# The first sub-layer of a two-layer decoder trunk: where its adaLN shift and scale are computed, and in which order its weights are loaded

## The chip, the core and the metric

The kernel runs on one core of one Trainium2 chip. The time is the device time of one execution in microseconds (us): 1291.8 us, the median of 3 runs (1289.95 to 1295.27). The core has a matrix engine (PE in the profile; its weight loads are shown apart as PEld), VectorE (DVE), ScalarE (ACT), GpSimd (POOL) and SyncE (SP), which here only issues loads. Each engine takes its own list of instructions, written when the kernel is built, and semaphores tie the lists together.

## The reference, cut to what matters

```python
c_act = jax.nn.silu(c)                                   # c: (1, 1024)
for l in range(2):
    mod = (c_act @ mod_w[l] + mod_b[l]).reshape(Bsz, 9, 1024)
    h = rmsnorm(x, norm_g[l, 0]) * (1.0 + mod[:, 1]) + mod[:, 0]
    g, u = split(h @ ffn_w13[l, 0]); y = (silu(g) * u) @ ffn_w2[l, 0]      # 2816 wide
    x = x + 0.5 * mod[:, 2] * rmsnorm(y, norm_g[l, 1])
    # then token mixing with mod 3, 4, 5 and a second such FFN with mod 6, 7, 8
```

x is 256 tokens by 1024 features, all in float32. For this change only the first FFN of layer 0 counts: the norm, the shift and scale of each feature (two columns of 1024 out of a product with a 1024 x 2048 piece of `mod_w`), and the first projection.

## The kernel before, in words

A float32 product is made of three fp32r products: a weight tile `raw` (128 x 2048, 1 MB) is split into two units, each a rounded part `hi` (ACT, line 164) and a rest `lo` (DVE, line 165), and `mm3` (lines 170 to 172) multiplies hi with the high part of the activations, lo with the same, and hi with their low part. The activations stand feature by token in `hT[0]` and `hT[1]`, in eight blocks of 128 features, called k = 0 to 7 below.

In the first FFN of layer 0 nothing lies ahead that could hide the start, and `first_chunks` (line 391) runs it block by block. Both token tiles are normed (lines 269 and 253: squares on ACT, a power on POOL, a product on DVE) and transposed on PE (line 400) into `xT`. Then, for each k, `mod_step` advances the generator `mod_cols`: 1 MB of `mod_w` is loaded, two SCALAR_TENSOR_TENSOR on DVE (line 189) multiply it by `crow`, the activated c spread over 128 partitions, and sum along the row, and two small instructions (191 and 192) finish the two columns `mcol` of the block. The block is modulated on DVE (411), rounded on ACT (412) and its rest taken on DVE (413). After that come all products that have become possible: four chunks (c0 to c3) of 512 gate and up columns are open at once, each with two loads (features 0 to 511 and 512 to 1023). The table `AFTER` says behind which k each of the eight loads is issued. The four chunks make 8 x 4 x 2 x 3 = 192 PE products called `gu`. `crow` is made ahead of everything: tanh on ACT (140), two DVE instructions (141 and 142), two PE products with a row of ones (146), two copies (147).

All loads of `mod_w` and of weights share one pool of three `raw` buffers. What stands where on each engine is decided by a scheduler that orders the instructions by its own estimates; SP's list is ordered in that way too. After the first four chunks the FFN goes on chunk by chunk, with PE as the busy engine and the modulation of later sub-layers strewn between.

Of the kernel before, what the change touches and what calls it, by code (L numbers as in the profile page):

```python
# [22 lines left out]
NT = 2  # L23
# [16 lines left out]
PEND_AT = 4  # L40
MSTEP0 = (0, 1, 2, 4, 1, 2, 1, 2)
MSTEP = (2, 2, 1, 1, 1, 1, 1, 1, 1)
AFTER = (0, 0, 2, 3, 4, 5, 6, 6)
N0 = 4
S2 = 9
MIX_STEP = (2, 1, 1, 1, 0, 0, 0, 0, 1, 2, 2, 2)

# [27 lines left out]
def trunk(ctx: ExitStack, tc: tile.TileContext, order, x_in, c_in, wst, smalls, gmws, ng_rows, modb, lnrows, rope_c, mask_c, out):  # L75
# [60 lines left out]
    A.activation(cth, view["cT"], AF.Tanh, scale=0.5)  # L136
    V.scalar_tensor_tensor(out=cact, in0=cth, scalar=1.0, in1=view["cT"], op0=ALU.add, op1=ALU.mult)
    V.tensor_scalar(cact, cact, 0.5, None, op0=ALU.mult)
    crow2 = s4("crow2", (1, D))
    A.activation(crow2, crow1, AF.Tanh, scale=0.5)  # L140
    V.scalar_tensor_tensor(out=crow2, in0=crow2, scalar=1.0, in1=crow1, op0=ALU.add, op1=ALU.mult)
    V.tensor_scalar(crow2, crow2, 0.5, None, op0=ALU.mult)
    crow = cp.tile([P, D], F32, name="crow")
    for h in range(2):
        pt = t_tile("crow")
        T.matmul(pt, lhsT=ones_r[0:1].bitcast(F32), rhs=crow2[:, h * 512 : (h + 1) * 512], start=True, stop=True)
        A.activation(crow[:, h * 512 : (h + 1) * 512], pt, AF.Copy)
# [29 lines left out]

    mods = {}

    def mod_cols(l, i):  # L180

        raw_c = cp.tile([P, 8, 2], F32, name="mraw", tag="mraw", bufs=2)
        o = cp.tile([P, 8, 2], F32, name="mcol", tag="mcol", bufs=2)
        mods[(l, i)] = o
        mb = view["mbT"][:, (l * 3 + i) * 16 : (l * 3 + i + 1) * 16].rearrange("p (j k) -> p k j", j=2)
        for k in range(8):
            raw = load(("modT", l, i, k))
            for j in range(2):
                V.scalar_tensor_tensor(out=raw[:, j * D : (j + 1) * D], in0=raw[:, j * D : (j + 1) * D], scalar=1.0, in1=crow, op0=ALU.mult, op1=ALU.mult, accum_out=raw_c[:, k, j : j + 1])  # L189
            if l == 0 and i == 0:  # L190
                V.tensor_tensor(o[:, k], raw_c[:, k], mb[:, k], ALU.add)
                V.scalar_tensor_tensor(out=o[:, k, 1:2], in0=o[:, k, 1:2], scalar=1.0, in1=view["ngT"][:, k : k + 1], op0=ALU.add, op1=ALU.mult)
            if k < 7:
                yield
        if not (l == 0 and i == 0):
            V.tensor_tensor(o, raw_c, mb, ALU.add)
            V.scalar_tensor_tensor(out=o[:, :, 1], in0=o[:, :, 1], scalar=1.0, in1=view["ngT"][:, (l * 3 + i) * 8 : (l * 3 + i + 1) * 8], op0=ALU.add, op1=ALU.mult)
        yield

    def mod_gate(l, i):  # L200
# [144 lines left out]
    def ffn(l, f, hT, pend, nxt):  # L345
# [45 lines left out]
        def first_chunks():  # L391

            xT = [s4("xT", (P, 4, S)) for _ in range(2)]
            xn = [norm(t) for t in range(NT)]
            for h in range(2):
                for t in range(NT):
                    pt = t_tile("xT")
                    for i in range(4):
                        k = 4 * h + i
                        T.transpose(out=pt[:, i * P : (i + 1) * P], in_=xn[t][:, k * P : (k + 1) * P], identity=ident)  # L400
                    A.activation(xT[h][:, :, t * P : (t + 1) * P], pt.rearrange("p (k q) -> p k q", k=4), AF.Copy)
            outs = [[m_tile("gu") for _ in range(NT)]] + [y_tile("gu") for _ in range(2)] + [[t_tile("gu") for _ in range(NT)]]
            us = [[] for _ in range(N0)]
            done = set()
            for k in range(8):
                mod_step()
                for c in [n for n in range(2 * N0) if AFTER[n] == k]:
                    us[c % N0] += units(("w13", l, f, c % N0, c // N0))
                mc = mods[(l, 0)]
                x32 = xT[k // 4][:, k % 4]  # L410
                V.tensor_scalar(x32, x32, mc[:, k, 1:2], mc[:, k, 0:1], op0=ALU.mult, op1=ALU.add)
                A.activation(hT[0][:, k], x32, AF.Copy)  # L412
                V.tensor_tensor(hT[1][:, k], x32, hT[0][:, k].bitcast(F32), ALU.subtract)  # L413
                ready = [(k2, c) for c in range(N0) for k2 in range(k + 1) if len(us[c]) > k2 // 2 and (k2, c) not in done]
# [20 lines left out]
            return pms[i, t]  # L435

        if pend is None:
            first_chunks()
            n0 = N0
        else:  # L440
            first_two(ps, [chunk_units(0), chunk_units(1)], (512, 512), hT, pend)
            for i in range(2):
                gate_t(1, pms[i, 1], st[i])
            n0 = 2
            mod_step(2)
# [41 lines left out]
    def mixing(l, hT, pend, nxt):  # L487
# [455 lines left out]

        return finish(down, y, mods[(l, 1, "g")], nxt)

    for t in range(NT):
        nc.sync.dma_start(x_t[t], x_in[0, t * P : (t + 1) * P, :])
    jobs.append(mod_cols(0, 0))
    hT, pend = hT_tiles(), None
    for l in range(L):  # L950
        if l > 0:
            jobs.extend([mod_gate(l, 0), mod_cols(l, 1)])
        hT, pend = ffn(l, 0, hT, pend, (l, 1))
        if l == 0:
            nc.sync.dma_start(sml[:, early:], smalls[:, early:])
            nc.sync.dma_start(rope.rearrange("p a t d -> p (a t d)"), rope_c)
            nc.sync.dma_start(mask, mask_c)
# [87 lines left out]
```

## Time and profile before

| | |
|---|---|
| median of 3 runs | 1291.8 us (1289.95 to 1295.27) |
| the profiled execution | 1292.15 us, of which its span, first to last instruction, is 1290.4 us |
| PE busy | 1254.8 us, 97% of the span, 5922 records |
| DVE busy | 1028.6 us, 80% |
| ACT busy | 680.9 us, 53% |
| DMA | 304.30 MB, mean 236 GB/s |

Times inside the span are counted from its first instruction. A record of the timeline begins with its start and its length; the idle time of the engine ahead of it and what ended that stands in brackets. Matmuls are pipelined, so the distance from one start to the next tells what one costs, not its length.

### The profile page before, as it was taken

Reading aid. Unit: us, or ns where it says so; the run is one execution under the profiler, and the core shown is the slowest. Engines: PE = TensorE matmul, PEld = TensorE weight load, DVE = VectorE, ACT = ScalarE, POOL = GpSimd, SP = SyncE. Lnnn points to the kernel's source line nnn. Section 1 sums busy time; section 2 is a strip of 40 time slices with the busy share of each in tenths; the row PEclk is TensorE's granted clock in tenths of the full one; section 3 lists DMA queues with packets and bytes.
Section 4 is the critical chain, followed back from the end, with each engine's and each line's share of the span. In section 5 each row is a group of like instructions: output and inputs, shape, how many; then the busy total and the mean of one; then the engine's idle time right before and its main releaser. Section 6 shows DMA issues by size and latency. Waiting matters only on the chain.

```text
span 1290.4 us, 15916 instructions
## 1 busy us (share of the span) xinstructions
PE 1254.8 (97%) x5922; PEld 1027.5 (80%) x5922; DVE 1028.6 (80%) x1632; ACT 680.9 (53%) x1129; POOL 31.6 (2%) x56
## 2 busy tenths in 40 slices
PE   6999999999999999999999999998999999999998
PEld 4788888778778878888878888887877887888886
DVE  7977997789999699767598767587999996875553
ACT  5454446476565464544465444456666574554442
POOL 1000001000000010000010000000000000100000
PEclk8999999999999999999999999999999999999999
DMA  8966885665466548767559767367535763684540
GB/s 328 362 234 248 325 325 193 228 236 186 173 264 238 224 180 326 283 240 292 196 180 350 276 252 272 141 236 285 191 133 224 293 264 132 260 308 170 184 168 33
DMA packets 43904, 304.30 MB, mean 236 GB/s; under 512 B 5169, under 2 KB 5425, under 8 KB 8498
## 3 DMA queue, kind: packets, MB, share of 16 engines
q1 hardware_dynamic: 43634, 303.26, 62.6%
q8 instruction: 46, 0.75, 0.2%
q14 instruction: 32, 0.26, 0.1%
q0 software_dynamic: 192, 0.02, 0.0%
HBM read 302.21 MB, written 1.05 MB: 235 GB/s over the span
## 4 chain that ended last, share of the span: by engine, by line
PE 75%; DVE 12%; ACT 5%; issue 4%; DMA 2%; POOL 1%; DVEq 0%; SPq 0%; POOLq 0%; ACTq 0%
PE gu L172 11%; PE gu L170 11%; PE gu L171 11%; PE yf L172 5%; PE yf L170 5%; PE yf L171 5%; DVE lo L165 3%; PE gt L171 3%; PE gt L172 2%; PE gt L170 2%; ACT hi L164 2%; DMA raw<-w_dram 2%; PE hT L363 2%; DVE raw L189 1%; PE xT L285 1%
## 5 line engine op out<-in xcount | busy, mean ns | idle before, releaser
L165 DVE TENSOR_TENSOR lo<-raw,hi 128x1024 fp32r<-128x1024 f32 (+1 forms) x416 | 495.9, 1210 | 104.4 <-ACT hi L164 100.9
L164 ACT ACTIVATE hi<-raw 128x1024 fp32r<-128x1024 f32 (+1 forms) x416 | 424.9, 1049 | 225.3 <-DMA raw<-w_dram 110.8
L170 PE MATMUL gu<-hi,hT 128*128 128x512 f32 x704 | 278.9, 397 | 4.3 <-ACT hT L412 4.3
L171 PE MATMUL gu<-lo,hT 128*128 128x512 f32 x704 | 275.5, 391 | 1.5 <-DVE lo L165 1.5
L172 PE MATMUL gu<-hi,hT 128*128 128x512 f32 x704 | 275.7, 392 | 0.0
L170 PEld LDWEIGHTS gu<-hi,hT 128*128 128x128 f32 x704 | 132.8, 189 | 31.9 <-ACT hT L412 4.5
L172 PEld LDWEIGHTS gu<-hi,hT 128*128 128x128 f32 x704 | 132.7, 189 | 29.7 <-DVE hT L413 0.7
L171 PEld LDWEIGHTS gu<-lo,hT 128*128 128x128 f32 x704 | 132.9, 189 | 28.9 <-DVE lo L165 2.4
L170 PE MATMUL yf<-hi,hid 128*128 128x512 f32 x352 | 137.6, 391 | 0.0
L171 PE MATMUL yf<-lo,hid 128*128 128x512 f32 x352 | 137.2, 390 | 0.0
L172 PE MATMUL yf<-hi,hid 128*128 128x512 f32 x352 | 137.0, 389 | 0.0
L355 ACT ACTIVATE ht<-gu 128x256 f32<-128x256 f32 x88 | 33.5, 384 | 159.4 <-PE gu L172 159.3
L189 DVE SCALAR_TENSOR_TENSOR raw<-raw,crow 128x1024 f32<-128x1024 f32 x96 | 115.2, 1217 | 2.4 <-DMA raw<-w_dram 1.9
L356 DVE SCALAR_TENSOR_TENSOR ht<-ht,gu 128x256 f32<-128x256 f32 x88 | 36.3, 416 | 60.7 <-ACT ht L355 60.6
L170 PE MATMUL gt<-hi,hT 128*128 128x512 f32 x192 | 76.3, 401 | 0.8 <-ACT th L598 0.8
L172 PEld LDWEIGHTS yf<-hi,hid 128*128 128x128 f32 x352 | 66.1, 188 | 13.7
L171 PE MATMUL gt<-lo,hT 128*128 128x512 f32 x192 | 75.7, 396 | 1.2 <-DVE lo L165 1.1
L171 PEld LDWEIGHTS yf<-lo,hid 128*128 128x128 f32 x352 | 66.1, 188 | 13.5
L170 PEld LDWEIGHTS yf<-hi,hid 128*128 128x128 f32 x352 | 66.1, 188 | 13.5
L172 PE MATMUL gt<-hi,hT 128*128 128x512 f32 x192 | 75.2, 393 | 0.0
L208 DVE SCALAR_TENSOR_TENSOR acc<-raw,cact,acc 128x1024 f32<-128x1024 f32 x48 | 61.4, 1279 | 1.3 <-DMA raw<-w_dram 0.9
L171 PEld LDWEIGHTS gt<-lo,hT 128*128 128x128 f32 x192 | 36.1, 188 | 10.3 <-DVE lo L165 3.6
(297 smaller groups left out, 1770.6 us busy)
## 6 DMA issues: line engine op xcount, KB each, us to landing
raw<-w_dram SPq DMA_DIRECT2D x276, 1024.0 KB, 4.8
raw<-w_dram SPq DMA_DIRECT2D x4, 816.0 KB, 4.2
gate<-ng_dram SPq DMA_DIRECT2D x6, 512.0 KB, 4.8
raw<-w_dram SPq DMA_DIRECT2D x4, 768.0 KB, 4.6
x<-x_dram SPq DMA_DIRECT2D x2, 512.0 KB, 4.6
ln<-ln_dram SPq DMA_DIRECT2D x2, 512.0 KB, 5.9
ws<-gmws_dram SPq DMA_DIRECT2D x2, 256.0 KB, 5.2
out_dram<-x SPq DMA_DIRECT2D x1, 512.0 KB, 2.6
```

The source lines that it names most:

```text
L164: A.activation(hi[:, :width], src, AF.Copy)
L165: V.tensor_tensor(lo[:, :width], src, hi[:, :width].bitcast(F32), ALU.subtract)
L170: T.matmul(o, lhsT=xh, rhs=wh, start=start, stop=False)
L171: T.matmul(o, lhsT=xh, rhs=wl, start=False, stop=False)
L172: T.matmul(o, lhsT=xl, rhs=wh, start=False, stop=stop)
L189: V.scalar_tensor_tensor(out=raw[:, j * D : (j + 1) * D], in0=raw[:, j * D : (j + 1) * D], scalar=1.0, in1=crow, op0=ALU.mult, op1=ALU.mul ...
L208: V.scalar_tensor_tensor(out=acc, in0=raw[:, u * D : (u + 1) * D], scalar=cact[:, k : k + 1], in1=acc, op0=ALU.mult, op1=ALU.add)
L285: T.transpose(out=pt[:, i * P : (i + 1) * P], in_=xn[:, k * P : (k + 1) * P], identity=ident)
L355: A.activation(h, pm[:, :256], AF.Tanh, scale=0.5)
L356: V.scalar_tensor_tensor(out=h, in0=h, scalar=1.0, in1=pm[:, :256], op0=ALU.add, op1=ALU.mult)
L363: T.transpose(out=pt[:, k * S + t * P : k * S + (t + 1) * P], in_=st[j]["h"][:, t, k * P : (k + 1) * P], identity=ident)
```

## The change

Four things are done, all in the first sub-layer of layer 0.

Blocks k = 0 and 1 take their two columns from PE: the generator `mod_first` replaces `mod_cols` there, and for k below `N_PE` = 2 it issues 16 float32 products (line 204 of the new kernel) with a 128 x 128 piece of `mod_w` as the stationary operand and one column of the activated c (`cact`) as the moving one. `mod_w` comes in two halves of 512 KB from the pool `s4` (14 buffers of 512 KB, shared by the whole kernel) and no longer through the three `raw` buffers. The first block's halves are loaded ahead of x. The loads follow each other as written, one pair of `mod_w` halves and one weight load per k (`AFTER` = 0 to 7), because SP's list is taken out of the scheduler's hands. `crow` is built later, behind the transposes. The squares of the second token tile go from ACT to one DVE instruction (line 425), and the modulation of a block goes from DVE to an ACT Identity (line 449).

```diff
-AFTER = (0, 0, 2, 3, 4, 5, 6, 6)
+AFTER = (0, 1, 2, 3, 4, 5, 6, 7)
+N_PE = 2
...
+    def spread_c():            # the lines that stood ahead of load(), now called in first_chunks
...
+        for h, pt in enumerate(y_tile("crow")):
+            T.matmul(pt, lhsT=ones_r[0:1].bitcast(F32), rhs=crow2[:, h * 512 : (h + 1) * 512], start=True, stop=True)
+            A.activation(crow[:, h * 512 : (h + 1) * 512], pt, AF.Copy)
...
+    def load_halves(desc):
+        i = len(order)
+        order.append(desc)
+        res = [s4("mw", (P, D)) for _ in range(2)]
+        for j in range(2):
+            nc.sync.dma_start(res[j], wst[i, :, j * D : (j + 1) * D])
+        return res
...
+    def mod_first(w0):
...
+        for k in range(8):
+            w = w0 if k == 0 else load_halves(("modP" if k < N_PE else "modT", 0, 0, k))
+            if k < N_PE:
+                src = y_tile("mc", 1)[0][:, 0:2]
+                for j in range(2):
+                    for kc in range(8):
+                        at = (kc % 4) * 256 + j * P
+                        T.matmul(src[:, j : j + 1], lhsT=w[kc // 4][:, at : at + P], rhs=cact[:, kc : kc + 1], start=kc == 0, stop=kc == 7)
+            else:
...
+                    V.scalar_tensor_tensor(out=w[j], in0=w[j], scalar=1.0, in1=crow, op0=ALU.mult, op1=ALU.mult, accum_out=src[:, j : j + 1])
+            V.tensor_tensor(o[:, k], src, mb[:, k], ALU.add)
+            V.scalar_tensor_tensor(out=o[:, k, 1:2], in0=o[:, k, 1:2], scalar=1.0, in1=view["ngT"][:, k : k + 1], op0=ALU.add, op1=ALU.mult)
+            yield
...
-            xn = [norm(t) for t in range(NT)]
+            mod_step()
+            sq = sm("ssy", [P, 2])
+            V.scalar_tensor_tensor(out=s4("sqj", (P, D)), in0=x_t[1], scalar=1.0, in1=x_t[1], op0=ALU.mult, op1=ALU.mult, accum_out=sq[:, 0:1])
+            xn = [norm(0), s4("xn", (P, D))]
+            V.tensor_scalar(sq[:, 1:2], sq[:, 0:1], 1.0 / D, EPS, op0=ALU.mult, op1=ALU.add)
+            G.tensor_tensor(sq[:, 1:2], sq[:, 1:2], mhalf[:, 0:1], ALU.pow)
+            V.tensor_scalar(xn[1], x_t[1], sq[:, 1:2], None, op0=ALU.mult)
...
+            spread_c()
...
             for k in range(8):
-                mod_step()
+                if k > 0:
+                    mod_step()
...
-                V.tensor_scalar(x32, x32, mc[:, k, 1:2], mc[:, k, 0:1], op0=ALU.mult, op1=ALU.add)
+                A.activation(x32, x32, AF.Identity, scale=mc[:, k, 1:2], bias=mc[:, k, 0:1])
...
-            first_chunks()
+            with tc.manual_schedule(engines={mybir.EngineType.SP}):
+                first_chunks()
...
+    w0 = load_halves(("modP", 0, 0, 0))
     for t in range(NT):
         nc.sync.dma_start(x_t[t], x_in[0, t * P : (t + 1) * P, :])
-    jobs.append(mod_cols(0, 0))
+    jobs.append(mod_first(w0))
```

Three places of the built lists matter below. Numbers behind a name tell buffers apart: `x0` and `x1` are the two token tiles, `mc_117` and `mc_215` the products of blocks 0 and 1 on PE, `gu_203` and `gu_204` chunk c0 for the two token tiles. The first place is the head of DVE's list. Before, the norm of both token tiles (`rxv`, `xn`) and `crow` stand first:

```order
L141 SCALAR_TENSOR_TENSOR crow2_102<-crow2_102,crow1_77 1x1024
L137 SCALAR_TENSOR_TENSOR cact_97<-cth_98,sml_76 128x8
L245 TENSOR_SCALAR rxv_124<-ssx_119 128x1
L142 TENSOR_SCALAR crow2_102<-crow2_102 1x1024
L138 TENSOR_SCALAR cact_97<-cact_97 128x8
L246 SCALAR_TENSOR_TENSOR rxv_124<-ssx_119,rxv_124 128x1
L245 TENSOR_SCALAR rxv_137<-ssx_132 128x1
L276 TENSOR_SCALAR xn_129<-x0_80,rxr_127 128x512 x2
```

In the changed kernel's DVE list the columns of block 0 (`mcol`, read from the PE product `mc`) stand ahead of the norm:

```order
L138 SCALAR_TENSOR_TENSOR cact<-cth,sml 128x8
L139 TENSOR_SCALAR cact<-cact 128x8
L209 TENSOR_TENSOR mcol<-mc,sml 128x2
L210 SCALAR_TENSOR_TENSOR mcol<-mcol,sml 128x1
L274 TENSOR_SCALAR rxv<-ssx 128x1
L275 SCALAR_TENSOR_TENSOR rxv<-ssx,rxv 128x1
L425 SCALAR_TENSOR_TENSOR sqj,ssy<-x_81 128x1024
L305 TENSOR_SCALAR xn<-x_80,rxr 128x512 x2
L427 TENSOR_SCALAR ssy<-ssy 128x1
L429 TENSOR_SCALAR xn<-x_81,ssy 128x1024
```

What moved: two instructions that wait for PE have come ahead of the first norm instruction, the second tile's squares stand between the two norms, and `crow` has gone to a place further on.

The second place is PE's list behind the transposes. Before, the `gu` products of block 0 (chunk c0, then c1) are followed by those of block 1:

```order
L170 MATMUL gu_169<-hi_187,hT0_115 128x512
L171 MATMUL gu_169<-lo_188,hT0_115 128x512
L170 MATMUL gu_170<-hi_187,hT0_115 128x512
L172 MATMUL gu_169<-hi_187,hT1_116 128x512
L171 MATMUL gu_170<-lo_188,hT0_115 128x512
L172 MATMUL gu_170<-hi_187,hT1_116 128x512
L170 MATMUL gu_171<-hi_197,hT0_115 128x512
```

In the changed kernel's PE list the six of block 0 are followed by the two `crow` products and the 16 of block 1:

```order
L180 MATMUL gu_203<-hi_192,hT0_109 128x512
L181 MATMUL gu_203<-lo_193,hT0_109 128x512
L180 MATMUL gu_204<-hi_192,hT0_109 128x512
L182 MATMUL gu_203<-hi_192,hT1_110 128x512
L181 MATMUL gu_204<-lo_193,hT0_109 128x512
L182 MATMUL gu_204<-hi_192,hT1_110 128x512
L148 MATMUL crow_184<-crow2_180,ones_r_89 128x512
L148 MATMUL crow_185<-crow2_180,ones_r_89 128x512
L204 MATMUL mc_215<-cact_97,mw_211 128x1 x4
L204 MATMUL mc_215<-cact_97,mw_212 128x1 x4
```

and on its DVE list everything of blocks 1 and 2 stands behind the `mcol` that reads `mc_215` (`lo_193` and `lo_197` are of chunk c0, `lo_237` and `lo_241` of c1):

```order
L175 TENSOR_TENSOR lo_193<-raw_190,hi_192 128x1024
L175 TENSOR_TENSOR lo_197<-raw_190,hi_196 128x1024
L145 SCALAR_TENSOR_TENSOR crow2_180<-crow2_180,crow1_77 1x1024
L451 TENSOR_TENSOR hT1_110<-xT_113,hT0_109 128x256
L146 TENSOR_SCALAR crow2_180<-crow2_180 1x1024
L209 TENSOR_TENSOR mcol_115<-mc_215,sml_76 128x2
L210 SCALAR_TENSOR_TENSOR mcol_115<-mcol_115,sml_76 128x1
L451 TENSOR_TENSOR hT1_110<-xT_113,hT0_109 128x256
L175 TENSOR_TENSOR lo_237<-raw_234,hi_236 128x1024
L175 TENSOR_TENSOR lo_241<-raw_234,hi_240 128x1024
L208 SCALAR_TENSOR_TENSOR mw_267,mraw_116<-mw_267,crow_102 128x1024
L208 SCALAR_TENSOR_TENSOR mw_268,mraw_116<-mw_268,crow_102 128x1024
```

What moved: `crow` and the product of block 1 now stand on PE between the `gu` of block 0 and of block 1, and DVE's list goes on only when PE has made that product.

The third place is ACT's list, blocks 2 and 3. Before, both `hi` of a load stand ahead of the block's rounding `hT0`, and nothing on ACT reads `mcol`:

```order
L164 ACTIVATE hi_249<-raw_247 128x1024
L164 ACTIVATE hi_253<-raw_247 128x1024
L412 ACTIVATE hT0_115<-xT_117 128x256
L164 ACTIVATE hi_298<-raw_296 128x1024
L164 ACTIVATE hi_302<-raw_296 128x1024
```

In the changed kernel's ACT list the Identity (L449) that reads `mcol` stands ahead of the `hi` of block 2 and behind those of block 3:

```order
L449 ACTIVATE xT_113<-xT_113,mcol_115 128x256
L174 ACTIVATE hi_277<-raw_275 128x1024
L174 ACTIVATE hi_281<-raw_275 128x1024
L450 ACTIVATE hT0_109<-xT_113 128x256
L174 ACTIVATE hi_330<-raw_328 128x1024
L174 ACTIVATE hi_334<-raw_328 128x1024
```

What moved: the modulation is on ACT's list now, and in blocks 2, 4 and 6 both `hi` stand behind it (in 3, 5 and 7 they stand ahead). On SP the loads stand from block 1 on as two halves of `mod_w`, one weight load, two halves, and so on to the end of the stage.

## Rows read from the trace of the kernel before

**Rows 1.** The page: busy time, share of the span, records

```profile
PE 1254.8 (97%) x5922; PEld 1027.5 (80%) x5922; DVE 1028.6 (80%) x1632; ACT 680.9 (53%) x1129; POOL 31.6 (2%) x56
```

**Rows 2.** Stretches: us, busy of PE, PEld, DVE, ACT, POOL, granted clock, DMA share, GB/s

```profile
0.00:18.83 18.83, 7.11 (x21) 3.94 (x21) 11.26 (x22) 12.55 (x22) 3.79 (x14) 0.96 0.80 311
18.83:24.40 5.57, 5.55 (x12) 3.94 (x13) 5.46 (x11) 0.42 (x1) 0.00 (x0) 0.51 0.95 369
24.40:52.00 27.60, 26.11 (x113) 20.70 (x112) 26.74 (x50) 11.83 (x16) 0.00 (x0) 1.00 0.94 356
52.00:66.80 14.80, 14.80 (x67) 12.25 (x66) 12.68 (x23) 8.76 (x14) 0.00 (x0) 1.00 0.93 363
66.80:120.00 53.20, 53.20 (x246) 44.06 (x245) 37.03 (x47) 23.86 (x31) 0.00 (x0) 1.00 0.60 216
```

**Rows 3.** Timeline of PE, 7 to 25 us: start, length, record, idle before

```profile
7.43 3.75 PE L146 MATMUL crow<-crow,ones_r 1*128 1x512 f32 x4 [7.43 <-DVE rxv L246]
11.11 3.42 PE L400 MATMUL xT<-ident,xn 128*128 128x128 f32 x16
18.83 0.79 PE L170 MATMUL gu<-hi,hT 128*128 128x512 f32 x1 [4.29 <-ACT hT L412]
...
23.65 0.63 PE L171 MATMUL gu<-lo,hT 128*128 128x512 f32 x1
24.08 0.49 PE L172 MATMUL gu<-hi,hT 128*128 128x512 f32 x1
```

**Rows 4.** Timeline of DVE, 3 to 9 us

```profile
3.40 1.21 DVE L141 SCALAR_TENSOR_TENSOR crow<-crow,crow 1x1024 f32<-1x1024 f32 x1 [3.40 <-ACT crow L140]
...
6.55 0.15 DVE L245 TENSOR_SCALAR rxv<-ssx 128x1 f32<-128x1 f32 x1 [1.86 <-ACT junk L253]
6.62 0.67 DVE L142 TENSOR_SCALAR crow<-crow 1x1024 f32<-1x1024 f32 x1
...
8.17 0.88 DVE L276 TENSOR_SCALAR xn<-x,rxr 128x512 f32<-128x512 f32 x2
```

**Rows 5.** Timeline of DVE: one whole block, and the stage's last block

```profile
29.55 1.22 DVE L189 SCALAR_TENSOR_TENSOR raw<-raw,crow 128x1024 f32<-128x1024 f32 x1
...
31.96 0.16 DVE L191 TENSOR_TENSOR mcol<-mraw,sml 128x2 f32<-128x2 f32 x1
...
32.35 0.42 DVE L411 TENSOR_SCALAR xT<-xT,mcol 128x256 f32<-128x256 f32 x1
32.68 2.36 DVE L165 TENSOR_TENSOR lo<-raw,hi 128x1024 fp32r<-128x1024 f32 x2
34.95 0.42 DVE L413 TENSOR_TENSOR hT<-xT,hT 128x256 fp32r<-128x256 f32 x1
35.29 1.22 DVE L189 SCALAR_TENSOR_TENSOR raw<-raw,crow 128x1024 f32<-128x1024 f32 x1
...
59.78 0.42 DVE L413 TENSOR_TENSOR hT<-xT,hT 128x256 fp32r<-128x256 f32 x1
```

**Rows 6.** Timeline of ACT, 5 to 19 us

```profile
5.79 0.63 ACT L253 ACTIVATE junk<-x 128x512 bf16<-128x512 f32 x1 [2.33 <-DMA x<-x_dram]
...
13.61 1.05 ACT L164 ACTIVATE hi<-raw 128x1024 fp32r<-128x1024 f32 x1
14.56 1.08 ACT L401 ACTIVATE xT<-xT 128x512 f32<-128x512 f32 x2
...
18.35 0.42 ACT L412 ACTIVATE hT<-xT 128x256 fp32r<-128x256 f32 x1
```

**Rows 7.** Timeline of POOL: the power of the norm

```profile
7.59 0.55 POOL L248 TENSOR_TENSOR rxr<-rxv,mhalf 128x1 f32<-128x1 f32 x1 [5.83 <-DVE rxv L246]
```

**Rows 8.** Timeline of PE: float32 products of 30 columns; transposes after the stage

```profile
267.53 1.86 PE L787 MATMUL pc<-kcB,qT 128*128 128x30 f32 x16
...
73.16 0.93 PE L363 MATMUL hT<-ident,ht 128*128 128x128 f32 x7
```

**Rows 9.** A stretch in which the load queue is full (columns as in rows 2)

```profile
5.00:10.00 5.00, 2.56 (x3) 1.16 (x4) 2.19 (x9) 3.15 (x9) 1.35 (x3) 1.00 1.03 424
```

More of the change, by code (lines that the diff above doesn't have):

```diff
@@ L138, in trunk @@
     V.tensor_scalar(cact, cact, 0.5, None, op0=ALU.mult)
[L139 to L142, printed above, removed]
     crow = cp.tile([P, D], F32, name="crow")
[L144 to L147, printed above, removed]
+    def spread_c():
+        crow2 = s4("crow2", (1, D))
+        A.activation(crow2, crow1, AF.Tanh, scale=0.5)
+        V.scalar_tensor_tensor(out=crow2, in0=crow2, scalar=1.0, in1=crow1, op0=ALU.add, op1=ALU.mult)
+        V.tensor_scalar(crow2, crow2, 0.5, None, op0=ALU.mult)
+        for h, pt in enumerate(y_tile("crow")):
+            T.matmul(pt, lhsT=ones_r[0:1].bitcast(F32), rhs=crow2[:, h * 512 : (h + 1) * 512], start=True, stop=True)
+            A.activation(crow[:, h * 512 : (h + 1) * 512], pt, AF.Copy)
     def load(desc, cols=2048):
@@ L178, in trunk @@
     mods = {}
+    def mod_first(w0):
+        o = cp.tile([P, 8, 2], F32, name="mcol", tag="mcol", bufs=2)
+        mods[(0, 0)] = o
+        raw_c = cp.tile([P, 8, 2], F32, name="mraw", tag="mraw", bufs=2)
+        mb = view["mbT"][:, 0:16].rearrange("p (j k) -> p k j", j=2)
+        for k in range(8):
[7 more added lines that the diff above has]
+            else:
+                src = raw_c[:, k]
+                for j in range(2):
+                    V.scalar_tensor_tensor(out=w[j], in0=w[j], scalar=1.0, in1=crow, op0=ALU.mult, op1=ALU.mult, accum_out=src[:, j : j + 1])
+            V.tensor_tensor(o[:, k], src, mb[:, k], ALU.add)
+            V.scalar_tensor_tensor(out=o[:, k, 1:2], in0=o[:, k, 1:2], scalar=1.0, in1=view["ngT"][:, k : k + 1], op0=ALU.add, op1=ALU.mult)
+            yield
     def mod_cols(l, i):
@@ L189, in mod_cols @@
                 V.scalar_tensor_tensor(out=raw[:, j * D : (j + 1) * D], in0=raw[:, j * D : (j + 1) * D], scalar=1.0, in1=crow, op0=ALU.mult, op1=ALU.mult, accum_out=raw_c[:, k, j : j + 1])
-            if l == 0 and i == 0:
-                V.tensor_tensor(o[:, k], raw_c[:, k], mb[:, k], ALU.add)
-                V.scalar_tensor_tensor(out=o[:, k, 1:2], in0=o[:, k, 1:2], scalar=1.0, in1=view["ngT"][:, k : k + 1], op0=ALU.add, op1=ALU.mult)
             if k < 7:
                 yield
-        if not (l == 0 and i == 0):
-            V.tensor_tensor(o, raw_c, mb, ALU.add)
-            V.scalar_tensor_tensor(out=o[:, :, 1], in0=o[:, :, 1], scalar=1.0, in1=view["ngT"][:, (l * 3 + i) * 8 : (l * 3 + i + 1) * 8], op0=ALU.add, op1=ALU.mult)
+        V.tensor_tensor(o, raw_c, mb, ALU.add)
+        V.scalar_tensor_tensor(out=o[:, :, 1], in0=o[:, :, 1], scalar=1.0, in1=view["ngT"][:, (l * 3 + i) * 8 : (l * 3 + i + 1) * 8], op0=ALU.add, op1=ALU.mult)
         yield
@@ L401, in first_chunks @@
                     A.activation(xT[h][:, :, t * P : (t + 1) * P], pt.rearrange("p (k q) -> p k q", k=4), AF.Copy)
-            outs = [[m_tile("gu") for _ in range(NT)]] + [y_tile("gu") for _ in range(2)] + [[t_tile("gu") for _ in range(NT)]]
+            spread_c()
+            makers = [lambda: [m_tile("gu") for _ in range(NT)]] + [lambda: y_tile("gu")] * 2 + [lambda: [t_tile("gu") for _ in range(NT)]]
+            outs = {}
             us = [[] for _ in range(N0)]
@@ L418, in first_chunks @@
                     done.add((k2, c))
+                    if c not in outs:
+                        outs[c] = makers[c]()
                     hi, lo = us[c][k2 // 2]
@@ L437, in ffn @@
         if pend is None:
-            first_chunks()
+            with tc.manual_schedule(engines={mybir.EngineType.SP}):
+                first_chunks()
+                nc.sync.dma_start(sml[:, early:], smalls[:, early:])
+                nc.sync.dma_start(rope.rearrange("p a t d -> p (a t d)"), rope_c)
+                nc.sync.dma_start(mask, mask_c)
             n0 = N0
@@ L953, in trunk @@
         hT, pend = ffn(l, 0, hT, pend, (l, 1))
[L954 to L957, printed above, removed]
         jobs.extend([mod_gate(l, 1), mod_cols(l, 2)])
@@ L1001, in pack @@
             put(i, [kt(inp["mod_w"][l], 2 * d[3] + k)[:, D * d[2] : D * d[2] + D] for k in range(2)])
+        elif kind == "modP":
+            w = inp["mod_w"][l]
+            put(i, [kt(w, k)[:, D * (3 * d[2] + j) + P * d[3] : D * (3 * d[2] + j) + P * d[3] + P] for k in range(8) for j in range(2)])
         else:
```

## The prediction, made before the changed kernel ran

> **What bounds the kernel now.** I read the page first. PE is busy for 97% of the span and the next engine for 80% [rows 1], so a change pays only where PE stands still or runs slowly. The table of stretches shows where that is. Until 18.83 us PE works 7.11 us; from there to 24.40 it makes 12 products at half clock; to 52.00 it makes 113 and is idle for 27.60 - 26.11 = 1.5 us; to 66.80 it makes 67 without a gap; and from there to 120 it is busy for all of 53.20 us [rows 2]. The 12, 113 and 67 are the 192 `gu` products of the four open chunks, so for PE the stage that is changed ends at 66.8, and what moves that point moves the end of the kernel: no idle time follows that could take it up. In the middle stretch DVE is busy for 26.74 of 27.60 us [rows 2], so the stage runs at DVE's pace. Its timeline gives one block, from 29.55 to 35.29: 2.41 for the two sums over `mod_w`, 0.39 for the two small ones, 0.33 for the modulation, 2.27 for two `lo`, 0.34 for the rest of the activations, 5.74 in all [rows 5]. The last block's rest starts at 59.78 and ends at 60.2 [rows 5]; behind it stand 24 products.
>
> One more thing is to be seen at DVE's head. The second `crow` instruction had its input at 3.40 + 1.21 = 4.61, but ran at 6.62, right behind an instruction that waited for ACT until 6.55 [rows 4]. An instruction that waits holds up all that stands behind it on its engine, and the changed lists put two such waits in front of DVE's work.
>
> **The change, part by part.** Loads. x0 lands at 5.8 now [rows 6]. Two halves of `mod_w`, 1.05 MB, go ahead of it; at 424 GB/s [rows 9] that is 2.5 us, so the halves are in at 5.8 and 7.0, x0 at 8.3 (its two squares on ACT done at 9.6) and x1 at 9.5. All that the stage loads is 17 MB of weights and x and 0.5 MB for a gate, 18.4 MB: in by 47 us at 424 GB/s, by 55 at 356 [rows 2], while DVE will want the last of it near 70. The order of loads therefore costs nothing after x0, and is worth nothing where DVE is later than the data.
>
> Block 0 on PE. A written float32 product leaves two records: 8 of them, with the same 128 x 128 stationary operand and 30 columns, leave 16, 0.116 us apart [rows 8]. No row shows one column; the weight load sets the distance, so I take it as equal. At the low clock I take the transposes at the start, 3.42 / 16 = 0.214 [rows 3], against 0.11 for the same shape later ((0.93 - 0.27) / 6) [rows 8]; the granted clock reads 0.96 there [rows 2], but the distances say the 1.2 GHz level. So 32 records take 3.7 us at 2.4 GHz or 6.8 at 1.2; PE has been idle, and I take 6.8: 5.8 + 6.8 = 12.6. (The Trainium skill, "TensorE: Matmul & The Clock Gate", section "LDWEIGHTS", gives columns divided by 1.2 as ns, an estimate of 107 ns for 128 columns at either clock. The trace is near it at the high level, with 0.116, and disagrees at the low one, with 0.214. By it block 0 would end before the squares and the sum below would be 3.3 us smaller.)
>
> The norm behind it. DVE's `mcol` stands ahead of `rxv`, so the norm starts at 12.7, not at 6.55 [rows 4]: 0.39 for `mcol`, 0.3 for two small ones, 1.2 for the squares of x1 (as the sums, 1.22 [rows 5]; POOL's 0.55 [rows 7] is hidden in it), 0.9 for xn0 [rows 4] make 15.5; a small one, POOL's power and the way there and back 0.9, and xn1 0.9 make 17.3. Then four transposes, 0.85, and on ACT, in its list's order, one `xT` 0.55, one `hi` 0.95, two `xT` 1.08, the tanh of `crow` (1024 columns, as a `hi`) 0.95, Identity 0.35 and `hT` 0.42 [rows 6]: the first `gu` starts at 22.5, not at 18.83 [rows 3].
>
> `crow` and block 1. Six `gu` at 0.43 (23.65 to 24.08) [rows 3] end at 25.1. `crow` took 3.75 us at the low level [rows 3], 1.9 at the high one. Before, the level rose 5.25 us after the first `gu` (18.83 to 24.08, where the distances change) [rows 3]; taking the same, it rises at 27.75, when 2.65 of the 3.75 are done; the rest ends at 28.3, and block 1's 32 records, now at 0.116, at 32.0. Bounds from the same rows: with the high level all along 1.3 + 1.9 + 3.7 = 6.9 us from the first `gu`, with the low one 2.6 + 3.75 + 6.8 = 13.2; I take 9.5. In all that time DVE has only c0's two `lo` and `crow`'s two instructions, and then waits. The four sums that it is spared (2.41 a block) would have fitted in there.
>
> Blocks 1 to 7. From 32.1: `mcol` 0.4, Identity and `hT` 0.7, the first `hi` of c1 1.0, so c1's `lo` start at 34.2 and end at 36.5. Six blocks follow at 5.74 - 0.33 = 5.41 (the modulation is ACT's), 32.5. In blocks 2, 4 and 6 both `hi` stand behind the Identity, which waits for `mcol`: DVE then waits for 0.35 + 0.95 and a little, 1.4 each, 4.2. The last block is ready at 73.2. Moving the seventh load from block 6 to block 7 leaves 42 products behind it, not 24; at 14.80 / 67 = 0.221 [rows 2] they take 9.3, and the stage ends at 82.5.
>
> The rest (a POOL memset that moves, SP's issues, four small loads) lies beside DVE's work and costs nothing; if the memset met a DVE instruction it would be under 1 us.
>
> Sum: 82.5 - 66.8 = 15.7 us later. The profiled execution took 1292.15 us, 0.35 over the median, so 1307.9 on its scale and 1307.5 on the median's. The change takes some 4.8 us of sums and 2.6 of modulation off DVE, and gives more than that back in waits for PE and ACT.
>
> **The rivals.** (1) PE is at the high level from the start. For it: the granted clock reads 0.96 up to 18.83 [rows 2]. Against: the distances of 0.214 [rows 3]. Then block 0 ends before x0's squares and the norm starts at 9.7, 3.0 earlier; the six `gu` and `crow` take 3.2 instead of 5.8. That is 5.6 less: +10.1, 1302.
>
> (2) PE stays at the low level until block 1 is done, because one-column products and one-row `crow` don't bring the clock up. For it: at the start 3.2 us of `crow` products ran without the level rising, since the transposes behind them still stand 0.214 apart [rows 3]. Then `crow` takes 0.5 more and block 1 3.1 more: +19.3, 1311.
>
> (3) Not slower: DVE's relief comes through. The mechanism is that PE makes both blocks' products early, in its idle time before 18.8 [rows 2], DVE reaches `mcol` later than they are done, and PE is then fed without a gap. From 18.83 PE took 47.97 us for 192 products; without the 1.5 us of gaps and without the 2.9 us that the low clock cost (5.57 - 12 x 0.221) [rows 2], but with `crow` 1.9 and block 1 3.7 in between, that is 49.2: +1.2, 1293. It decides from the point where PE's six `gu`, `crow` and block 1 together are shorter than what DVE has to do meanwhile (c0's two `lo`, `crow`, block 0's rest, 2.3 + 1.9 + 0.3 = 4.5 us); against it stand 6.9 us even at the high level, and PE's list. To be 0.5% (6.5 us, about what a measurement can tell from no change) faster, `gu` would have to start some 6 us before 18.83, but x0 alone lands 2.5 us later and before it took 13.0 us from x0's landing (5.79) to the first `gu` [rows 3, 6].
>
> **How the numbers follow.** The forecast has a chance of 0.57, with its own range of 1304 to 1311; rival 1 0.20, rival 2 0.13, rival 3 0.10. The range from 1299 to 1313 takes in rivals 1 and 2 with some error of mine, and leaves out rival 3 and a few per cent beyond 1313. Slower by over 0.5% begins at 1298.3: the first three cases without 0.03 at rival 1's low end, 0.87. Within 0.5%: that 0.03 and 0.07 of rival 3, 0.10. Faster: 0.03.
>
> **What would show it.** In the changed profile: x0's squares on ACT start near 8.3; the first `rxv` on DVE stands idle until PE's block 0 is done, near 12.7; the first `gu` starts near 22.5; between the sixth and the seventh `gu` lie `crow` and block 1, some 7 us, with DVE idle most of that; DVE's distance from block to block is 5.4, and 6.8 in blocks 2, 4 and 6 with idle time ended by ACT's `hi`; behind the last `hT` rest stand 9 us of `gu`; PE is full from there on. I am wrong if the first `gu` comes before 19, if DVE doesn't wait for block 1, or if the records of one-column products stand much closer than 0.11 us.

## The result and the profile after

The changed kernel takes 1308.38 us, the median of 4 runs (1308.02 to 1309.99), against 1292.43 us of the kernel before beside it: slower by a ratio of 1.013, 95% interval 1.0114 to 1.0146. In medians that is 15.95 us; the two profiled executions (1309.99 and 1292.15 us) lie 17.8 apart.

Only the first 85 us differ. The page reads as before [rows 1], with DVE busy for 7 us less:

```profile
PE 1266.2 (97%) x5986; PEld 1039.3 (79%) x5986; DVE 1022.0 (78%) x1616; ACT 684.9 (52%) x1133; POOL 32.5 (2%) x56
```

The table of stretches (length; busy time of PE, PEld, DVE, ACT, POOL; granted clock; DMA share; GB/s), cut where the one of before was cut [rows 2] and once more at the end of the stage:

```profile
0.00:18.83 18.83, 8.84 (x40) 8.39 (x41) 3.73 (x12) 4.33 (x8) 3.06 (x12) 1.00 0.86 318
18.83:24.40 5.57, 2.91 (x12) 2.18 (x11) 4.17 (x5) 4.39 (x8) 0.00 (x0) 1.00 1.01 421
24.40:52.00 27.60, 24.57 (x95) 18.91 (x94) 14.93 (x25) 9.83 (x14) 0.00 (x0) 0.81 0.65 238
...
66.80:85.20 18.40, 16.93 (x73) 13.73 (x74) 15.55 (x28) 12.05 (x19) 0.00 (x0) 1.00 0.39 128
85.20:120.00 34.80, 34.80 (x163) 28.92 (x162) 22.66 (x27) 17.43 (x22) 0.00 (x0) 1.00 0.70 255
```

DVE, busy before for 26.74 of the 27.60 us of the third stretch [rows 2], is busy for 14.93: the engine that set the pace now waits. PE's last gap in the stage ends at 69.0; from there on it is full. PE's timeline, to set beside [rows 3]:

```profile
6.38 6.96 PE L204 MATMUL mc<-cact,mw 128*128 128x1 f32 x32 [6.38 <-DMA mw<-w_dram]
...
23.64 0.80 PE L180 MATMUL gu<-hi,hT 128*128 128x512 f32 x1 [2.66 <-ACT hT L450]
...
26.50 2.06 PE L148 MATMUL crow<-crow,ones_r 1*128 1x512 f32 x4
28.48 5.55 PE L204 MATMUL mc<-cact,mw 128*128 128x1 f32 x32
35.56 0.80 PE L180 MATMUL gu<-hi,hT 128*128 128x512 f32 x1 [1.52 <-ACT hT L450]
```

And DVE's, to set beside [rows 4, 5]: the two waits for the one-column products, the squares that now stand behind the first of them, a wait for ACT's `hi`, and the last rest of the stage.

```profile
13.37 0.16 DVE L209 TENSOR_TENSOR mcol<-mc,sml 128x2 f32<-128x2 f32 x1 [9.54 <-PE mc L204]
...
13.97 1.22 DVE L425 SCALAR_TENSOR_TENSOR sqj<-x 128x1024 f32<-128x1024 f32 x1
...
34.07 0.16 DVE L209 TENSOR_TENSOR mcol<-mc,sml 128x2 f32<-128x2 f32 x1 [9.24 <-PE mc L204]
...
43.14 2.36 DVE L175 TENSOR_TENSOR lo<-raw,hi 128x1024 fp32r<-128x1024 f32 x2 [1.62 <-ACT hi L174]
...
75.29 0.42 DVE L451 TENSOR_TENSOR hT<-xT,hT 128x256 fp32r<-128x256 f32 x1
```

Counted in the timeline, the 192nd `gu` ends at 85.16; counted the same way it ended at 67.73 before (the stretches put it at 66.8). That is 17.4 us, and the profiled executions differ by 17.8: the whole loss is made in this stage and nothing is given back later (from there to the end of the span it is 1223.1 us, and 1222.7 before).

The granted clock shows what the prediction didn't foresee. A table of stretches cut at its changes:

```profile
6.40:13.30 6.90, 6.90 (x32) 6.85 (x32) 0.00 (x0) 1.33 (x4) 0.00 (x0) 1.00 1.02 400
26.70:30.10 3.40, 3.40 (x19) 2.15 (x19) 0.00 (x0) 1.20 (x2) 0.00 (x0) 1.00 0.99 413
30.10:40.30 10.20, 8.68 (x30) 7.63 (x31) 4.56 (x8) 2.91 (x4) 0.00 (x0) 0.50 0.19 48
```

Ahead of the first change that the trace records the column reads 1.00 and tells nothing: 32 records in 6.96 us are 0.217 apart, the distance of the 1.2 GHz level [rows 3]. From 26.7 to 30.1 the level is 2.4 GHz, and at 30.1, in the middle of block 1's one-column products, with PE busy all the time, it falls to 1.2 GHz and stays there until 40.3.

### The profile page after: what moved, and what is told of

Its sections match the earlier page's. It is cut to its first block, busy times and chain, and to the rows that moved or that the text cites. A ratio compares the mean times of both kernels' runs of the same rounds, so it can differ in the third digit from the quotient of the medians.

```text
span 1308.3 us, 16031 instructions
## 1 busy us (share of the span) xinstructions
PE 1266.2 (97%) x5986; PEld 1039.3 (79%) x5986; DVE 1022.0 (78%) x1616; ACT 684.9 (52%) x1133; POOL 32.5 (2%) x56
## 4 chain that ended last, share of the span: by engine, by line
PE 74%; DVE 11%; ACT 6%; issue 4%; DMA 2%; POOL 1%; DVEq 0%; POOLq 0%; ACTq 0%
PE gu L180 11%; PE gu L182 11%; PE gu L181 11%; PE yf L180 5%; PE yf L181 5%; PE yf L182 5%; DVE lo L175 3%; DMA raw<-w_dram 2%; ACT hi L174 2%; PE gt L181 2%; PE gt L182 2%; PE gt L180 2%; PE hT L392 1%; DVE mw L208 1%; PE xT L314 1%
## 5 line engine op out<-in xcount | busy, mean ns | idle before, releaser
L222 DVE SCALAR_TENSOR_TENSOR raw<-raw,crow 128x1024 f32<-128x1024 f32 x80 | 96.3, 1218 | 2.3 <-DMA raw<-w_dram 2.3
L385 DVE SCALAR_TENSOR_TENSOR ht<-ht,gu 128x256 f32<-128x256 f32 x88 | 36.5, 418 | 59.5 <-ACT ht L384 59.4
```

The lines of the kernel that those rows point to most:

```text
L385: V.scalar_tensor_tensor(out=h, in0=h, scalar=1.0, in1=pm[:, :256], op0=ALU.add, op1=ALU.mult)
```

## The experiments

Theory: the loss has three parts. PE's one-column products stand in the path (ahead of the norm, and again between the first `gu` and block 1); `crow` now stands there too; and the new table with the Identity on ACT costs the rest, as waits for `hi` and as products left behind the last block. The rival to the first part is that a single thing (the place of `mcol`, one of the two blocks, the table, or the clock) carries most of it. All edits are made to the changed kernel unless the text says otherwise. Each ratio is to runs of the kernel before that were taken beside the run (medians 1291.03 to 1292.94); the times of the stage are those of one trace for each run, in us (`mc` 1: block 1's products on PE; level: where the last low stretch at the head ends, behind which the `gu` stand at 2.4 GHz distances; e_npe0, e_npe1 and e_pin have one more low stretch of 3.4 us in the second half of the stage):

| run | median | ratio to before, 95% | first gu | mc 1 | level | last rest ends | 192nd gu ends |
|---|---|---|---|---|---|---|---|
| before | 1292.43 | 1 | 18.83 | | 24.3 | 60.20 | 67.73 |
| after | 1308.38 | 1.0130 [1.0114, 1.0146] | 23.64 | 28.48 to 34.03 | 40.3 | 75.71 | 85.16 |
| e_npe0 | 1298.30 | 1.0041 [1.0025, 1.0057] | 19.79 | | 26.0 | 63.02 | 74.09 |
| e_combo0 | 1293.51 | 1.0007 [0.9993, 1.0021] | 21.91 | | 26.3 | 60.23 | 68.70 |
| e_npe1 | 1308.88 | 1.0122 [1.0097, 1.0147] | 23.79 | | 39.8 | 73.34 | 84.41 |
| e_pin | 1308.82 | 1.0112 [1.0080, 1.0145] | 20.12 | 26.14 to 33.13 | 37.9 | 74.81 | 85.87 |
| e_after | 1306.55 | 1.0108 [1.0079, 1.0138] | 25.47 | 34.76 to 41.58 | 46.1 | 76.06 | 85.23 |
| e_dve | 1307.86 | 1.0116 [1.0098, 1.0135] | 23.34 | 29.91 to 36.89 | 42.9 | 75.92 | 84.94 |
| e_wide | 1299.28 | 1.0057 [1.0044, 1.0071] | 22.51 | 25.24 to 29.48 | 26.3 | 68.15 | 76.10 |
| w_after | 1306.02 | 1.0117 [1.0098, 1.0136] | 24.43 | 25.92 to 29.55 | 36.4 | 71.22 | 80.67 |
| w_wide_after | 1297.70 | 1.0046 [1.0031, 1.0061] | 22.73 | 28.02 to 31.78 | 28.1 | 65.87 | 74.11 |
| b_d | 1294.38 | 1.0015 [1.0006, 1.0024] | 15.78 | | 33.5 | 59.48 | 69.97 |
| w_before | 1291.68 | 1.0007 [0.9995, 1.0020] | 17.37 | | 30.0 | 61.22 | 68.40 |

**No block on PE (e_npe0).**

```diff
-N_PE = 2
+N_PE = 0                 # and w0 in the layout of the other blocks
-            spread_c()   # behind the transposes
+    spread_c()           # ahead of load(), as before
```

> The changed kernel with no block on PE (N_PE = 0) and crow made ahead of the norm, as before; everything else as changed (loads, AFTER, Identity on ACT, squares of x1 on DVE). Theory (waits of DVE for PE): both waits go, DVE does 4.8 us more of sums, the first gu comes near 19 to 20, and 9 to 12 us of the 16 come back: 1297 to 1300. Rival (the table, the Identity and x's later landing cost it, not the products): under 4 us come back, 1305.

11.1 of the stage's 17.4 us come back (85.16 to 74.09), 10 in the medians. The products with `crow` behind the transposes are the larger part of the loss. What is left is, for one thing, a wait that the changed kernel and this one share, here in this run:

```profile
30.44 2.36 DVE L177 TENSOR_TENSOR lo<-raw,hi 128x1024 fp32r<-128x1024 f32 x2 [1.61 <-ACT hi L176]
42.74 2.36 DVE L177 TENSOR_TENSOR lo<-raw,hi 128x1024 fp32r<-128x1024 f32 x2 [1.62 <-ACT hi L176]
55.02 2.36 DVE L177 TENSOR_TENSOR lo<-raw,hi 128x1024 fp32r<-128x1024 f32 x2 [1.62 <-ACT hi L176]
```

Three waits of 1.6 are 4.8 us, for 8 modulations of 0.33 that DVE is spared, 2.6: the last rest ends 2.8 later than before. Behind it stand 11.1 us of `gu`, not 7.5. Not all of that is the table's: behind the third of these waits PE, which stood idle for it too, makes some 8 `gu` at the low level. Its timeline and the stretch:

```profile
55.05 0.73 PE L182 MATMUL gu<-hi,hT 128*128 128x512 f32 x2 [1.69 <-ACT hi L176]
```

```profile
56.70:60.10 3.40, 3.40 (x10) 2.66 (x9) 3.37 (x7) 1.44 (x2) 0.00 (x0) 0.50 0.52 140
```

At 0.427 us apart and not 0.227 they cost 1.6 us, and since PE is full from there on, they move the stage's end by as much. The changed kernel's trace has the same wait (1.70 us up to 67.74) and no fall behind it.

**And the old table, and the modulation on DVE (e_combo0).**

```diff
-AFTER = (0, 1, 2, 3, 4, 5, 6, 7)
+AFTER = (0, 0, 2, 3, 4, 5, 6, 6)
-                A.activation(x32, x32, AF.Identity, scale=mc[:, k, 1:2], bias=mc[:, k, 0:1])
+                V.tensor_scalar(x32, x32, mc[:, k, 1:2], mc[:, k, 0:1], op0=ALU.mult, op1=ALU.add)
```

> Only the loads' order, their pool, and the squares of x1 on DVE are left of the change: no block on PE, crow ahead of the norm, old AFTER, modulation on DVE. Theory: DVE's work is that of the kernel before plus 1.2 us of squares and the norm 2.5 us later; time within 3 us of the kernel before, 1292 to 1295. Rival (the new order of loads itself costs): over 1297.

The last rest ends at 60.23 as before (60.20), and the time is the time before. So the new order of loads, the halves from the shared pool and x1's squares on DVE cost and bring nothing that can be measured, and the two parts make up nearly the whole: 11.1 and 5.4 of the 17.4 us in the stage, or some 12.7 and 3.8 without the 1.6 us of low level in e_npe0's trace; in the medians 10.1 and 4.8.

**One thing undone at a time (e_npe1, e_pin, e_after, e_dve).** In turn: one block on PE only; block 0's `mcol` held behind both norms in DVE's list; the old table; the modulation on DVE (the last two as in the diff above, each alone).

```diff
-N_PE = 2
+N_PE = 1                 # e_npe1, and nothing else
```

```diff
-            mod_step()
             sq = sm("ssy", [P, 2])
...
             V.tensor_scalar(xn[1], x_t[1], sq[:, 1:2], None, op0=ALU.mult)
+            mod_step()   # e_pin; its first DVE instruction is kept in program order
```

> The changed kernel with N_PE = 1: only block 0 on PE, block 1 by DVE's two sums again. Theory (waits): crow is still made between the gu of blocks 0 and 1, so DVE waits for it till 29.2 and then needs 2.7 for the two sums and mcol: block 1's mcol near 32 instead of 34.1, and the kernel some 2 us faster, 1306. Rival (clock): without one-column products behind it the granted clock stays at 1.0 from 26.7 on, the 10.2 us at 0.5 are gone and with them up to 5 us, 1303.

> The changed kernel with one instruction moved on DVE: block 0's mcol stands behind both norms and no longer ahead of the first, so the norm does not wait for PE's block 0. Theory (DVE's list waits): the norm starts at 10.2, when x0's squares are done, and not at 13.6; the first gu comes 2 to 3 us earlier, near 21; the stage's end moves by about as much less what crow and block 1 on PE take back, so 1306 to 1307. Rival (the low clock costs it): clock rows unchanged, no gain, 1308. Rival (x comes 2.5 us later because mod_w is loaded first): no gain, 1308.

> The changed kernel with the old table AFTER = (0, 0, 2, 3, 4, 5, 6, 6). Theory: 24 instead of 42 gu stand behind the last block, 18 x 0.227 = 4 us less, and the second load at block 0 gives DVE two lo to do while it waits for block 1 (2.3 us that then lie beside the wait): 4 to 6 us faster, 1303. Rival (clock alone): 1308.

> The changed kernel with the modulation on DVE again (TENSOR_SCALAR instead of ACT's Identity). Theory (waits): three waits of 1.6 us for a hi behind the Identity go, 6 x 0.33 us of modulation come back on DVE, so 2.8 us less: 1305 to 1306. Rival (relief of DVE counts, its waits don't): 2 us more, 1310.

All four bring 0 to 2 us in the medians (1 to 3 by the ratios), no more than their intervals are wide. The traces say why. What each saves is taken by the next wait in the same series, and by the clock: in all four `crow` runs at the low level, 3.78 us and not 2.06, and in the three that have block 1 on PE its products take 6.8 to 7.0, not 5.55. So the clock takes back up to 3 us, and what the parts are worth at one and the same level isn't shown. In e_pin the first `gu` comes 3.5 us earlier, but the level falls at 20.8 and block 1 is done only 0.9 earlier. In e_npe1 block 1's sums are on DVE, but wait for `crow`, done at 30.43; the last rest still ends 2.4 us earlier, and then 8 `gu` at the low level (67.1 to 70.5, behind the wait for `hi`, as in e_npe0) take 1.6 of that. e_pin loses as much from 68.6 to 72.0. In e_dve the waits for `hi` are gone, but block 1 is done 2.9 later and DVE has the modulations again. In e_after the earlier weights put 12 `gu` ahead of block 1's products, not 6, all at the low level:

```profile
26.20 3.78 PE L148 MATMUL crow<-crow,ones_r 1*128 1x512 f32 x4
29.90 0.80 PE L181 MATMUL gu<-lo,hT 128*128 128x512 f32 x1
...
34.34 0.63 PE L182 MATMUL gu<-hi,hT 128*128 128x512 f32 x1
34.76 6.82 PE L204 MATMUL mc<-cact,mw 128*128 128x1 f32 x32
41.44 1.20 PE L180 MATMUL gu<-hi,hT 128*128 128x512 f32 x2
```

Its last rest ends at the changed kernel's time although block 1 was done 7.5 us later: DVE made block 2's two sums (30.64 to 32.94) and two more `lo` in the meantime. A part undone alone tells little where another wait stands right behind it.

**The products 128 columns wide (e_wide).** The moving operand is the column of `cact` repeated 128 times; column 0 of each result is read.

```diff
...
-T.matmul(src[:, j : j + 1], lhsT=w[kc // 4][:, at : at + P], rhs=cact[:, kc : kc + 1], start=kc == 0, stop=kc == 7)
+T.matmul(wide[:, j * P : (j + 1) * P], lhsT=w[kc // 4][:, at : at + P], rhs=cact[:, kc : kc + 1].to_broadcast([P, P]), start=kc == 0, stop=kc == 7)
```

> The changed kernel with PE's products of blocks 0 and 1 made 128 columns wide (the same column of c repeated), all else as changed apart from where the scheduler puts the instructions around them. If one-column products don't count as work for the clock and let it fall, the granted clock is up during or right behind block 0 and does not fall during block 1: records of block 1 stand 0.11 us apart, 1.9 us less than 5.55, and block 1's gu run at full rate. If the clock falls whatever the width, block 1 takes as long as in the changed kernel. As to time: theory (waits): 2 us or what the other order brings; rival (clock): 5 us or more, 1303.

128 times the columns, and 9 us faster. PE's timeline:

```profile
5.72 5.48 PE L205 MATMUL mc<-cact,mw 128*128 128x128 f32 x32 [5.72 <-DMA mw<-w_dram]
...
19.11 3.46 PE L148 MATMUL crow<-crow,ones_r 1*128 1x512 f32 x4 [2.72 <-DVE crow L146]
...
25.24 4.24 PE L205 MATMUL mc<-cact,mw 128*128 128x128 f32 x32
```

The level rises at 9.2, within block 0, and again at 26.3, within block 1, where with one column block 0 stays at the low level and the level falls in block 1. But not all of the 9 us is the clock's: in this build `mcol` also stands behind the norm's first steps and x1's squares on DVE, and `crow` ahead of the first `gu`. The next two runs try to raise the level alone.

**PE kept busy at the head (w_after, w_wide_after).** Products of ones, read by nobody, fill PE's idle time; w_wide_after has the wide products and the old table as well. In both the fillers and block 0's products are kept in the order of the program.

```diff
+            T.matmul(pt[:, 0:P], lhsT=ones_r.bitcast(F32), rhs=ones_r.bitcast(F32), start=True, stop=True)
+    warm(12)      # ahead of block 0; 12 more behind it, 8 behind the transposes
```

> The changed kernel with products of 128 x 128 ones (their result is read by nobody) put into PE's idle time at the head: 12 ahead of block 0, 12 behind it, 8 behind the transposes. Theory A (the low level of the clock is a large part of what blocks 0 and 1 cost): block 0 takes 3.7 us instead of 6.96 and ends near 10.1, the first gu comes near 20 instead of 23.64, block 1 is done near 27 instead of 34.03, the last hT rest near 69, the stage ends near 78 instead of 85.2: 1301. If the one-column products of block 1 let the level fall again, the gu behind them run at half rate for some us and 1 to 3 us are lost: 1302 to 1304. Theory B (the level doesn't matter, since DVE and ACT set the pace): within 1 us of the changed kernel's 1308.4.

> As the run before it, with the products over mod_w 128 columns wide and the old table AFTER. Theory A: the level stays up through block 1, block 1 is done near 27, the last hT rest near 69, and 24 products stand behind it, not 42: the stage ends near 74, 1297. If the table is worth nothing even with the level up: 1301. Theory B: 1306, as the old table alone gave.

For w_after first, then for w_wide_after, a table of stretches with block 0 and then block 1, and PE's timeline (`crow` and block 1; block 1):

```profile
5.70:9.10 3.40, 2.99 (x26) 2.75 (x25) 0.00 (x0) 0.11 (x1) 0.00 (x0) 1.00 1.02 407
9.12:15.95 6.83, 6.83 (x33) 6.83 (x34) 2.93 (x10) 1.21 (x4) 1.94 (x2) 0.50 0.99 378
25.92:29.60 3.68, 3.62 (x33) 3.54 (x31) 0.02 (x1) 0.00 (x0) 0.00 (x0) 1.00 1.01 388
29.60:36.40 6.80, 5.33 (x13) 4.19 (x14) 5.13 (x8) 2.91 (x4) 0.00 (x0) 0.50 0.39 127
```

```profile
22.52 1.98 PE L155 MATMUL crow<-crow,ones_r 1*128 1x512 f32 x4 [0.93 <-DVE crow L153]
...
25.92 3.63 PE L211 MATMUL mc<-cact,mw 128*128 128x1 f32 x32
```

```profile
6.30:10.40 4.10, 4.00 (x33) 3.83 (x34) 0.15 (x1) 1.33 (x4) 0.00 (x0) 1.00 1.02 412
...
28.07:31.70 3.63, 3.63 (x34) 3.63 (x32) 0.00 (x0) 0.00 (x0) 0.00 (x0) 1.00 1.03 425
31.70:40.30 8.60, 7.74 (x33) 5.84 (x33) 6.75 (x13) 4.65 (x8) 0.00 (x0) 1.00 0.83 320
```

```profile
28.02 3.76 PE L212 MATMUL mc<-cact,mw 128*128 128x128 f32 x32
```

With one column the level falls during block 0 (at 9.1) and at the end of block 1 (at 29.6), though PE has no idle time within either; with 128 columns it holds through both. In w_after block 1 takes 3.63 us, the price that the prediction put on it; it is done 4.5 earlier than in the changed kernel, and that 4.5 reaches the stage's end (80.67 against 85.16). In the medians it is 2.4 us, and the intervals of the two ratios overlap, so the traces show it and the times alone don't. The fillers behind block 0 ran at the low level and held the transposes up to 16.43, and in this build `crow` stands ahead of the six `gu`, so the first `gu` was not earlier and the expected 1301 was missed, and 1302 to 1304 for a level that falls again too: 1306.02, with runs from 1303.98 to 1310.64. w_wide_after comes to 1297.70, where 1297 was expected, but by another way: block 1 is done at 31.78 (expected: near 27), the last rest ends at 65.87 (69), and 35 products start behind it (24). It is 8.9 below e_after, which has the same table. How much of that is the level's isn't shown, since `crow` stands ahead of the first `gu` in this build too and the norm's first step ahead of `mcol`; nor is it shown that the old table pays, as e_wide leaves 7.95 us of `gu` behind the last rest with the new one, and this run 8.24. Still, 6.4 us stay in the stage: 12 `gu` run at the low level between the two blocks (21.3 to 28.1), and two waits of 1.62 for `hi` are left. What the path through PE would cost without these no run shows.

**Two attempts at a faster kernel (b_d, w_before).** b_d has no block on PE, x and `crow` loaded first, the modulation on ACT behind both `hi`, and the engines' lists as written; w_before is the kernel before with products of ones in PE's idle time (14 ahead of `crow`, 6 and 14 around the transposes).

```diff
-AFTER = (0, 1, 2, 3, 4, 5, 6, 7)
+AFTER = (0, 0, 2, 3, 4, 4, 5, 6)      # b_d, with N_PE = 0
```

> A version meant to beat both: no block on PE, crow and x first as before, loads in order of need from the shared pool, Identity on ACT, and the lists of PE, DVE, ACT and SP in the order of the program, in which each block's mcol, Identity and hT stand ahead of the hi and lo not needed yet; AFTER = (0, 0, 2, 3, 4, 4, 5, 6). If the late start costs the kernel before its time (first gu at 18.83, here near 15.5), 3 us are gained: 1289. If DVE's rate of finishing blocks and lo decides the stage's end, the earlier start is given back as idle PE in blocks 1 to 3 and the time is that of the kernel before within 1.5 us.

> The kernel before with such products of ones in PE's idle time at the head: 14 ahead of crow, 6 ahead of the transposes, 14 behind them. If the level is up from the start, crow takes 1.9 us instead of 3.75 and the transposes 1.8 instead of 3.42, and the 12 gu at half rate are gone; but DVE sets the pace of the blocks, so only what its first block comes earlier counts, 2 to 3 us: 1290. If DVE's first block does not move, 0: 1292.4.

Neither beats the kernel before; b_d is 2 us slower. Its first `gu` is 3 us earlier, but PE waits 3.83 us at 26.56. In w_before `crow` takes 1.98 us, and the first `gu` is 1.5 us earlier, but then PE waits for DVE's second block:

```profile
7.11 1.98 PE L153 MATMUL crow<-crow,ones_r 1*128 1x512 f32 x4 [0.17 <-DVE crow L142]
...
20.79 0.40 PE L179 MATMUL gu<-hi,hT 128*128 128x512 f32 x1
24.70 0.80 PE L177 MATMUL gu<-hi,hT 128*128 128x512 f32 x1 [3.52 <-ACT hT L421]
```

So raising PE's clock at the head is worth nothing in w_before, where DVE sets the pace, and 4.5 us of the stage in w_after's trace, where the change puts PE into the path.

## Why the prediction came out right, point by point

The time was forecast at 1307.5 and is 1308.4; the mechanism was the forecast one. Within it one step failed, and some sizes were off.

- Loads: x0's squares start at 8.82 (forecast: near 8.3). Right to half a microsecond.
- Block 0 on PE: 32 records in 6.96 us at the low level (6.8), and DVE waits 9.54 us for them, with the norm behind. Right; e_pin shows that this wait alone set the first `gu`, by 3.5 us.
- First `gu` at 23.64, not 22.5: `mod_w` 0.6 later, and POOL's power took 1.39 us where [rows 7] had 0.55.
- The level of the clock: this is the step that failed. "It rises at 27.75" was near (26.7) by luck: it came 3.1 us behind the first `gu`, not 5.25, and the first `gu` was late. So `crow` took 2.0 us, not 3.2. But the forecast also let the level stay up, and block 1's records run 0.116 apart until 32.0. It fell at 30.1, so block 1 took 5.55 us, not 3.7, and was done at 34.03. The 1.2 us gained on `crow` hide most of the 1.85 lost on block 1: from the first `gu` to block 1's end it is 10.4, and 9.5 were forecast. Rival 2 had the reason in part (under one-column products the level doesn't come up); in this trace `crow`'s one-row products ran at the high level, 2.06 us, and in the four runs with one thing undone at the low one, 3.78. (Its 3.2 us of `crow` before are 3.75 in [rows 3].) w_after gives the term: with the level up block 1 takes 3.63.
- Blocks 1 to 7: c1's `lo` end at 38.8 (36.5); from there to the last rest 36.9 us against 36.7, with three waits of 1.62 (1.4; the Identity takes 0.6, not 0.35). Right.
- 42 products behind the last rest: 40 in the trace, 9.5 us (9.3). Right. But the 24 of before are 32 in its trace (60.20 to 67.73), since PE is still at products of earlier blocks there, so the table's move doesn't cost the 18 products that it seems to; e_after, with the old table, leaves 39.
- Sum in the trace: 17.4 us, not 15.7. The stage's end was put 2.7 too early (82.5, measured 85.16): 1.1 up to the first `gu`, 0.9 from there to block 1's end, 0.6 in small terms behind. The end before was put 0.9 too early as well (66.8, by the timeline 67.73): the table of stretches counts a product that crosses a bound in both stretches, so 12, 113 and 67 are three more than had been started by then. That the medians come so near, 15.95 apart, is luck in part: the changed kernel's profiled execution lies 1.6 above its median.

Rival 1 fell with 6.96 us for block 0. The relief of DVE (rival 3) is real, 12 us less busy in the third stretch, but DVE spends most of that waiting for PE (9.24 us for block 1). (The Trainium skill's "TensorE: Matmul & The Clock Gate", section "LDWEIGHTS", has a load's time by its columns alone, an estimate of 3.4 us for 32 loads of 128 columns. At the high level the distance is near that, 3.63 us for 32; at the low one it is 6.96 for 32, and the measurement decides.)

What stays open: no run separates the place of `crow` from the products themselves, and each run has one trace, so the level of the clock in its other executions, and how often it falls behind a wait for `hi`, is not known.

## What to carry to other kernels

Work that is moved from a busy engine to an idle one pays only if its result comes earlier than the busy engine would have made it: work out the new chain to the first consumer, with the instructions queued behind each wait. Where several waits stand in series, undo them together as well as one at a time; here four parts alone gave 0 to 2 us each, both blocks off PE with `crow` put back 10, and all of it 15. Where the clock's level differs between two runs, look at its rows before a difference of some us is put down to the edit.

## What the runs showed of the hardware that was not expected

PE can be busy without a gap and still lose its clock. With float32 products of one column the granted clock fell to 0.50 three times, during them or at their end, with PE full since their start at least (30.1 in the changed kernel, 9.1 and 29.6 in w_after), and block 0's records stayed at the low level for all their 6.96 us, in the changed kernel as in e_npe1, e_pin, e_after and e_dve. In e_dve PE is busy without a gap from 23.34 to 36.89 (six `gu`, `crow`, block 1), and by the distances it stays at the low level all that time. With 128 columns in the same products the level came up within block 0 (9.2, e_wide) and held (1.00 from 28.1 to 40.3, w_wide_after). The 32 records with 128 columns took hardly longer than with one: 3.76 against 3.63 us. (The Trainium skill, "TensorE: Matmul & The Clock Gate", "Part 1: The HAM clock gate", has the level follow how busy PE has been; here a PE that the profile shows as busy was not enough.)
